# Attention products in whole float32 on halves of the array, and the first stage's normalised x one step ahead

## The chip, the cores and the metric

The kernel runs on one NeuronCore of a Trainium2 chip. The metric is device time in microseconds of one execution, as the median of several; lower is better. Engines in the rows: PE is TensorE (matmuls), PEld its weight loads, DVE is VectorE, ACT is ScalarE, POOL is GpSimd, SP is SyncE, which here only issues transfers.

## The reference

A decoder trunk of two layers over 256 tokens of width 1024, all in float32. Each layer adds half a SwiGLU feed-forward (1024 to 2816 and back), then a mixer, then another half feed-forward; every part reads an RMS-normalised x.

```python
h = h + 0.5 * swiglu(rms_norm(h, ffn1_norm[layer]), ...)
hn = rms_norm(h, mix_norm[layer])
h = h + ab_mixer(hn, ...)        # layer 0:  c_mixer(hn, ...) in layer 1
h = h + 0.5 * swiglu(rms_norm(h, ffn2_norm[layer]), ...)
...
# c_mixer: 16 heads of 64, 256 tokens are one block, so plain causal attention
q, k, v = split(x @ w_in, 3)
p = softmax(where(kpos <= qpos, q @ k.T * 64 ** -0.5, -inf))
out = (p @ v) @ w_out
```

The mixer of layer 0 has 8 heads of 64 with three dilated windows, whose outputs are combined by their softmax denominators (with 256 tokens this is one softmax with a mask that holds the logarithm of how many windows see a key), and beside them a gated branch with 128x128 position mixing; both go through one output projection.

## The kernel before, in words

The work runs on TensorE as products of float32 numbers that are cut in two: `split(hi, lo, src)` lets ScalarE round `src` to float32r (line 228, `hi`) and VectorE subtract (line 229, `lo`). A product of two cut operands is three matmuls: hi by hi, hi by lo, lo by hi (`mm3`, lines 223 to 225, and written out in `rowwise`, lines 365 to 367, `colwise`, 375 to 377, and `project`, 423 to 427). `Stream` loads every weight once from memory on SyncE's queue as a tile `raw` of 128x2048, and cuts it into `whi` (ScalarE, line 91) and `wlo` (VectorE, line 92), two pieces a tile. Three raw and four cut tiles are in flight. PSUM is eight banks of 128x512, taken by `bank()`.

The phases follow each other: feed-forward (with `begin` as the start of the first), `ab_mixer`, feed-forward, feed-forward, `c_mixer`, feed-forward. Within a phase the tile planner orders the instructions of each engine by data dependence, the program's order and its own estimates of time; `begin` alone is run under `manual_schedule`, in the order written. In a mixer the projections for q and k are computed for two heads (a pair, 128 columns) at a time; `at(slot, f, h)` puts the attention steps of head h or pair p into numbered slots between those projections, and the last slots fall into the output projection (`project`'s `after`). Layer 0 has 4 pairs, layer 1 has 8.

The steps of attention, as `make_attention` has them:
- `put_q`: for each head of the pair, q is rounded by ScalarE (line 716) into the head's own 64 rows, and VectorE's remainder (717) goes to the other 64 rows of the same tile. So q high and q low lie above each other in 128 rows.
- `put_k`: k is rounded (727) and its remainder taken (728), and GpSimd copies both to the other 64 rows (729, 730), so that kh and kl each stand twice.
- `scores`: for each head and each block of 128 queries two matmuls over 128 rows, by kh (742) and by kl (743), give (q high + q low) times k. VectorE adds the mask and takes the minimum of the negated scores (746), ScalarE takes the exponential and its sum (748), and ScalarE (755, layer 0) or GpSimd (757, layer 1) scales by the reciprocal of the sum. Only the causal part is kept: 128 keys for the first block, 256 for the second.
- `turn`: three TensorE transposes (765) put the probabilities of a head with keys in rows, and a `split` gives `pth` and `ptl`.
- `weighted`: `mm3` with v's 128 columns of the pair as the held operand and both heads' probabilities as the moving one. Each head's result is the half of the output rows that belongs to it; the other half is not used. A `split` for each head writes `mixh` and `mixl`.

V is kept as `vth` and `vtl` after a `split` of its projection.

In `begin`, the first tokens' products are made with x times gain, not yet normalised, while the norms are computed. `normed` then makes the normalised x, two slices of 128 rows at a time: VectorE multiplies (line 575), then `split` rounds on ScalarE (228) and subtracts on VectorE (229). Behind it, on the same two engines, the next weight tile is cut. Ahead of it two `colwise` products with the unnormalised `xgh`, `xgl` are ready for TensorE.

Of the kernel before, what the change touches and what calls it, by code (L numbers as in the profile page):

```python
# [140 lines left out]
def trunk(ctx: ExitStack, tc: tile.TileContext, a, out):  # L141
# [12 lines left out]
    def bank():  # L154
        return ps.tile([128, 512], F32, name="bank")
# [71 lines left out]
    def split(hi, lo, src):  # L227
        nc.scalar.activation(hi, src, AF.Copy)
        nc.vector.tensor_sub(lo, src, hi.bitcast(F32))
# [258 lines left out]
    def begin(bp, fp, pb):  # L488
# [80 lines left out]
        rs = bp.tile([128, 2, S], F32, name="rs")  # L569
        new_xT()  # L570

        def normed(k0):
            for k in range(k0, k0 + 4, 2):
                for i in range(k, k + 2):
                    nc.vector.scalar_tensor_tensor(xf[:, i, :], xf[:, i, :], gT[:, i : i + 1], rs[:, 0, :],
                                                   op0=ALU.mult, op1=ALU.mult)
                xk = xf[:, k : k + 2, :].rearrange("p k (t c) -> p k t c", t=NT)
                split(xT["h"][:, k : k + 2], xT["l"][:, k : k + 2], xk)

        pair = []  # L580
        for _ in range(2):
# [1 line left out]
            st.load_one()  # L583
        for j in range(2):
            nc.scalar.copy(rs[:, j, :], rb[:, :S])
        for m in range(2):
            normed(4 * m)
        st.split_one()
        st.load_one()
        for m in range(2):  # L590
# [111 lines left out]


    def make_attention(mp, mask_cols, nheads, v, mix, engine):
        qs, ks, probs, pts = {}, {}, {}, {}
        mask = mp.tile([128, 384], F32, name="mask")
        nc.scalar.dma_start(mask, a["consts"][:, mask_cols])

        def put_q(p, bk):

            qq = mp.tile([128, 2 * S + LINE], F32R, name="q", bufs=PAIRS)
            for j in range(2):
                q = qq[:, SHIFT + j * S : SHIFT + (j + 1) * S]
                r = slice(j * 64, j * 64 + 64)
                o = slice(64 - j * 64, 128 - j * 64)
                nc.scalar.activation(q[r, :], bk[r, :S], AF.Copy)
                nc.vector.tensor_sub(q[o, :], bk[r, :S], q[r, :].bitcast(F32))
                qs[2 * p + j] = q

        def put_k(p, bk):  # L720

            for j in range(2):
                kh = mp.tile([128, S], F32R, name=f"kh{j}", bufs=PAIRS)
                kl = mp.tile([128, S], F32R, name=f"kl{j}", bufs=PAIRS)
                r = slice(j * 64, j * 64 + 64)
                o = slice(64 - j * 64, 128 - j * 64)
                nc.scalar.activation(kh[r, :], bk[r, :S], AF.Copy)
                nc.vector.tensor_sub(kl[r, :], bk[r, :S], kh[r, :].bitcast(F32))
                nc.gpsimd.tensor_copy(kh[o, :], kh[r, :].bitcast(F32))
                nc.gpsimd.tensor_copy(kl[o, :], kl[r, :].bitcast(F32))  # L730
                ks[2 * p + j] = (kh, kl)

        def scores(h):
            q = qs.pop(h)
            kh, kl = ks.pop(h)
            sc = bank()
            pr = mp.tile([128, 384], F32, name="pr", bufs=4)
            nm = wk.tile([128, 2], F32, name="nm")
            l = wk.tile([128, 2], F32, name="l")
            for b in range(2):  # L740
                bs = slice(b * 128, b * 128 + 128)
                nc.tensor.matmul(sc[:, b * S : (b + 1) * S], q[:, bs], kh, start=True, stop=False)
                nc.tensor.matmul(sc[:, b * S : (b + 1) * S], q[:, bs], kl, start=False, stop=True)
            for b, (c0, n) in enumerate(((0, 128), (128, 256))):
                cs = slice(c0, c0 + n)
                nc.vector.tensor_tensor_reduce(pr[:, cs], sc[:, b * S : b * S + n], mask[:, cs], -SCALE, 3e38,
                                               op0=ALU.add, op1=ALU.min, accum_out=nm[:, b : b + 1])
                nc.scalar.activation(pr[:, cs], pr[:, cs], AF.Exp, bias=nm[:, b : b + 1], scale=-1.0,
                                     accum_out=l[:, b : b + 1])
            rl = wk.tile([128, 2], F32, name="rl")  # L750
            nc.vector.reciprocal(rl, l)
            for b, (c0, n) in enumerate(((0, 128), (128, 256))):
                cs = slice(c0, c0 + n)
                if engine is nc.scalar:
                    nc.scalar.activation(pr[:, cs], pr[:, cs], AF.Copy, scale=rl[:, b : b + 1])
                else:
                    engine.tensor_scalar(pr[:, cs], pr[:, cs], rl[:, b : b + 1], None, op0=ALU.mult)
            probs[h] = pr

        def turn(h):  # L760
            p, j = divmod(h, 2)
            pr = probs.pop(h)
            tp = bank()
            for i in range(3):
                nc.tensor.transpose(tp[:, i * 128 : (i + 1) * 128], pr[:, i * 128 : (i + 1) * 128], ident)
            if j == 0:
                pts[p] = [mp.tile([128, 2, 384], F32R, name=n, bufs=2) for n in ("pth", "ptl")]
            split(pts[p][0][:, j, :], pts[p][1][:, j, :], tp[:, :384])

        def weighted(p):  # L770
            o = bank().rearrange("p (j c) -> p j c", j=2)
            pth, ptl = pts.pop(p)
            vs = slice(p * 128, (p + 1) * 128)
            mm3(o, v[0][:, 0, vs], v[1][:, 0, vs], pth[:, :, :256], ptl[:, :, :256], True, False)
            mm3(o[:, :, 128:], v[0][:, 1, vs], v[1][:, 1, vs], pth[:, :, 256:], ptl[:, :, 256:], False, True)
            for j in range(2):
                r = slice(j * 64, j * 64 + 64)
                split(mix[0][r, p], mix[1][r, p], o[r, j, :].rearrange("p (t c) -> p t c", t=NT))

        return put_q, put_k, scores, turn, weighted  # L780

    def mix_tiles(mp):
        return [mp.tile([128, KD, NT, 128], F32R, name=n) for n in ("mixh", "mixl")]

    def v_tiles(mp, n):
        return [mp.tile([128, NT, n], F32R, name=m) for m in ("vth", "vtl")]

    def run_events(ev, s):
        for f in ev.pop(s, []):
# [3 lines left out]
    def ab_mixer(phase):  # L793
        with tc.tile_pool(name="mp", bufs=1) as mp:
            mix = mix_tiles(mp)
            v = v_tiles(mp, 512)
            vn = mp.tile([128, NT, 512], F32, name="vn")
            uT = mp.tile([128, 4, S], F32, name="uT")
            put_q, put_k, scores, turn, weighted = make_attention(mp, slice(0, 384), 8, v, mix, nc.scalar)
# [28 lines left out]
                        st.free()  # L828

            def keep_v(t):  # L830
                split(v[0][:, t, :], v[1][:, t, :], pb[t, 0])

            def keep_g(t):
                g = mp.tile([128, 512], F32, name="gv")
# [74 lines left out]
    def c_mixer(phase):  # L909
        with tc.tile_pool(name="mp", bufs=1) as mp:  # L910
            mix = mix_tiles(mp)
            v = v_tiles(mp, D)
            put_q, put_k, scores, turn, weighted = make_attention(mp, slice(384, 768), 16, v, mix, nc.gpsimd)
            ws, pb = {}, {}

            def block(t, m, mid=None):
                pb[t, m] = bank()
                for i in range(2):
                    if t == 0:
                        ws[m, i] = st.take()  # L920
                    rowwise(pb[t, m], t, i * 4, ws[m, i], 4)
                    if t == 1:
                        st.free()
                    if mid:
                        mid()
                cs = slice(m * 512, (m + 1) * 512)
                split(v[0][:, t, cs], v[1][:, t, cs], pb[t, m])

            ev = {}
            slot = 0  # L930

            def at(s, f, *args):
                ev.setdefault(s, []).append(lambda: f(*args))

            def step():
                nonlocal slot
                run_events(ev, slot)
                slot += 1

            for h, s in enumerate((4, 5, 6, 8, 8, 10, 11, 12, 15, 16, 17, 18, 19, 20, 20, 21)):  # L940
                at(s, scores, h)
            for h, s in enumerate((6, 7, 8, 10, 11, 12, 13, 14, 17, 18, 19, 20, 22, 22, 22, 23)):
                at(s, turn, h)
            for p, s in enumerate((9, 12, 14, 16, 20, 22, 23, 23)):
                at(s, weighted, p)

            block(0, 0)
            pend[1].turn((nc.vector, nc.scalar))
            block(1, 0)
            for c in range(4):  # L950
                if c == 2:
                    block(0, 1, step)
                    block(1, 1, step)
                for put in (put_q, put_k):
                    w = st.take()
                    for j in range(2):
                        p = bank()
                        colwise(p[:, :S], w, j)
                        put(2 * c + j, p)
                        step()  # L960
                    st.free()
            project(mix, list(range(8)), 4, 1.0, phase + 1, lambda i: step())
            assert not ev, ev.keys()
# [58 lines left out]
```

## Time and profile before

| what | value |
|---|---|
| median of 3 runs | 943.3 us (943.08 to 946.66) |
| the profiled execution, its own time | 943.16 us |
| its span, first to last instruction | 941.4 us |
| granted TensorE clock | 0.999 |
| TensorE busy | 930.4 us, 99% |
| VectorE, ScalarE, GpSimd busy | 668.3, 543.5, 176.4 us |
| memory read | 173.73 MB, 186 GB/s over the span |

A row of instructions reads: line, engine, operation, tiles written and read, shapes, count, then total busy time and the mean of one in ns, then the engine's idle time before them and what ended it. A row of waits reads: who waited, for whom, total us, times, longest. A matmul's record covers its way through the array, so records of successive matmuls overlap; the distance between starts tells how long TensorE is held. Shapes such as 128*128 are the rows and columns of the array that are used.

### The profile page before, as it was taken

The numbers are of one execution on the slowest core, as the hardware profiler recorded it, in microseconds if no ns is written. First come the engines' busy times: TensorE is split into PE (matmuls) and PEld (weight loads), VectorE is DVE, ScalarE is ACT, GpSimd is POOL, SyncE is SP. The second block draws the span as 40 slices with busy tenths as digits, with TensorE's granted clock in tenths as the row PEclk, the third lists the DMA queues.
The fourth block names the chain that finished last, engine by engine and source line by source line (L and its number), as shares of the span: only waits on it lengthen the run. The fifth ranks groups of instructions, "written<-read, shape, count | busy, mean of one in ns | idle before, by whom it ended". The sixth has DMA issues, their size and how long they took to land.

```text
span 941.4 us, 15697 instructions
## 1 busy us (share of the span) xinstructions
PE 930.4 (99%) x6320; PEld 851.3 (90%) x6320; DVE 668.3 (71%) x927; ACT 543.5 (58%) x875; POOL 176.4 (19%) x201
## 2 busy tenths in 40 slices
PE   9999999999999999999999999999999999999997
PEld 8999998889878999988889999887999889999886
DVE  6786678768766566678665667787788666567785
ACT  6664554575976445545654545457787574455451
POOL 0013312011200023121001222200446200132210
PEclk9999999999999999999999999999999999999999
DMA  9786555566434756547466654574544438664531
GB/s 329 222 281 199 180 211 180 191 206 228 134 101 155 248 180 187 175 176 262 157 207 185 207 191 156 202 241 141 196 147 135 134 122 259 197 202 144 219 135 45
DMA packets 119464, 175.78 MB, mean 187 GB/s; under 512 B 3168, under 2 KB 92384, under 8 KB 119392
## 3 DMA queue, kind: packets, MB, share of 16 engines
q1 hardware_dynamic: 117712, 172.60, 55.6%
q10 hardware_dynamic: 1680, 2.19, 0.8%
q8 instruction: 49, 0.80, 0.3%
q14 instruction: 23, 0.19, 0.1%
HBM read 173.73 MB, written 1.05 MB: 186 GB/s over the span
## 4 chain that ended last, share of the span: by engine, by line
PE 88%; ACT 5%; DVE 3%; DMA 2%; issue 1%; SPq 0%; POOL 0%; POOLq 0%; ACTq 0%; DVEq 0%
PE bank L377 16%; PE bank L376 16%; PE bank L375 16%; PE bank L427 6%; PE bank L423 6%; PE bank L424 6%; PE bank L367 4%; PE bank L365 4%; PE bank L366 4%; PE bank L223 3%; PE bank L224 3%; PE bank L225 3%; DVE wlo L92 2%; DMA raw<-in_ffn_w_up 2%; ACT whi L91 2%
## 5 line engine op out<-in xcount | busy, mean ns | idle before, releaser
L91 ACT ACTIVATE whi<-raw 128x1024 fp32r<-128x1024 f32 (+1 forms) x336 | 328.6, 1026 | 230.6 <-PE bank L376 96.3
L92 DVE TENSOR_TENSOR wlo<-raw,whi 128x1024 fp32r<-128x1024 f32 (+1 forms) x336 | 391.7, 1205 | 79.8 <-ACT whi L91 78.9
L375 PE MATMUL bank<-xTh,whi 128*128 128x256 f32 x1344 | 372.7, 277 | 0.0
L377 PE MATMUL bank<-xTh,wlo 128*128 128x256 f32 x1344 | 371.5, 276 | 0.8 <-DVE wlo L92 0.8
L376 PE MATMUL bank<-xTl,whi 128*128 128x256 f32 x1344 | 371.4, 276 | 0.0
L377 PEld LDWEIGHTS bank<-xTh,wlo 128*128 128x128 f32 x1344 | 252.3, 188 | 1.0 <-DVE wlo L92 1.0
L376 PEld LDWEIGHTS bank<-xTl,whi 128*128 128x128 f32 x1344 | 252.6, 188 | 0.1
L375 PEld LDWEIGHTS bank<-xTh,whi 128*128 128x128 f32 x1344 | 252.4, 188 | 0.2 <-ACT whi L91 0.2
L423 PE MATMUL bank<-whi,hTh 128*128 128x512 f32 x216 | 84.7, 392 | 0.0
L424 PE MATMUL bank<-wlo,hTh 128*128 128x512 f32 x216 | 84.1, 389 | 0.0
L427 PE MATMUL bank<-whi,hTl 128*128 128x512 f32 x216 | 71.1, 389 | 0.0
L365 PE MATMUL bank<-whi,xTh 128*128 128x512 f32 x160 | 63.1, 394 | 0.0
L367 PE MATMUL bank<-whi,xTl 128*128 128x512 f32 x160 | 62.5, 390 | 0.0
L366 PE MATMUL bank<-wlo,xTh 128*128 128x512 f32 x160 | 62.3, 390 | 0.0
L663 POOL TENSOR_TENSOR sil<-hm 128x128 f32<-128x128 f32 x16 | 7.4, 463 | 279.7 <-DVE hm L622 239.0
L622 DVE TENSOR_TENSOR hm<-sil,bank 128x512 f32<-128x512 f32 x35 | 24.0, 685 | 49.5 <-PE bank L377 49.5
L99 POOL TENSOR_TENSOR wx<-raw 128x512 f32<-128x512 f32 x16 | 21.9, 1371 | 172.0 <-DVE wxl L92 87.0
L235 POOL TENSOR_TENSOR rstd<-ms,half_neg 128x1 f32<-128x1 f32 x14 | 12.4, 886 | 206.9 <-DVE ms L269 202.6
L427 PEld LDWEIGHTS bank<-whi,hTl 128*128 128x128 f32 x216 | 40.5, 188 | 8.5
L424 PEld LDWEIGHTS bank<-wlo,hTh 128*128 128x128 f32 x216 | 40.6, 188 | 8.2
L423 PEld LDWEIGHTS bank<-whi,hTh 128*128 128x128 f32 x216 | 40.6, 188 | 8.2
L91 ACT ACTIVATE wxh<-wx 128x1536 fp32r<-128x1536 f32 x16 | 23.7, 1483 | 25.3 <-DVE wx L103 21.6
(172 smaller groups left out, 1282.4 us busy)
## 6 DMA issues: line engine op xcount, KB each, us to landing
raw<-in_ffn_w_down SPq DMA_DIRECT2D x44, 1024.0 KB, 5.0
raw<-in_ffn_w_gate SPq DMA_DIRECT2D x41, 1024.0 KB, 5.4
raw<-in_ffn_w_up SPq DMA_DIRECT2D x41, 1024.0 KB, 5.4
raw<-in_c_w_in SPq DMA_DIRECT2D x12, 1024.0 KB, 5.3
raw<-in_ab_w_in SPq DMA_DIRECT2D x10, 1024.0 KB, 6.3
raw<-in_ab_w_out SPq DMA_DIRECT2D x4, 1024.0 KB, 4.9
raw<-in_c_w_out SPq DMA_DIRECT2D x4, 1024.0 KB, 5.0
raw<-in_ffn_w_up SPq DMA_DIRECT2D x6, 512.0 KB, 7.0
```

Of the source, the lines that this page charges most:

```text
L91: self.nc.scalar.activation(hi, raw, AF.Copy)
L92: self.nc.vector.tensor_sub(lo, raw, hi.bitcast(F32))
L223: nc.tensor.matmul(p, sh, mh, start=start, stop=False)
L365: nc.tensor.matmul(p, xh, w[0][:, k, :], start=k0 + k == 0, stop=False)
L366: nc.tensor.matmul(p, xh, w[1][:, k, :], start=False, stop=False)
L367: nc.tensor.matmul(p, xl, w[0][:, k, :], start=False, stop=k0 + k == KD - 1)
L375: nc.tensor.matmul(p, h, xh, start=k == 0, stop=False)
L376: nc.tensor.matmul(p, h, xl, start=False, stop=False)
L377: nc.tensor.matmul(p, l, xh, start=False, stop=k == KD - 1)
L423: nc.tensor.matmul(banks[t, h], sh, w[0][:, kw, cs], start=first, stop=False)
L424: nc.tensor.matmul(banks[t, h], sh, w[1][:, kw, cs], start=False, stop=False)
L427: nc.tensor.matmul(banks[t, h], sl, w[0][:, kw, cs], start=False, stop=last)
```

## The change

Attention keeps q, k, v and the probabilities as plain float32. `put_q` is one ScalarE copy of the pair, `put_k` one VectorE copy, v one VectorE copy, and a transposed head one ScalarE copy. `scores` issues the matmuls of both heads of a pair at the even head, into two banks: for each block of queries first the head in rows 0 to 63, then the head in rows 64 to 127, with 128 keys for the first block in place of 256. `weighted` issues, for each half of the keys, one matmul for each head, whose 64 columns of v give output rows 0 to 63 or 64 to 127 of the same bank; one `split` of full height follows. The slots stay as they were.

In `begin`, `normed` runs over all eight slices, and the `split` of one pair of slices is issued after the multiplies of the next pair.

```diff
-        def normed(k0):
-            for k in range(k0, k0 + 4, 2):
-                for i in range(k, k + 2):
+        def normed():
+            for k in range(0, KD + 2, 2):
+                for i in range(k, min(k + 2, KD)):
                     nc.vector.scalar_tensor_tensor(xf[:, i, :], xf[:, i, :], gT[:, i : i + 1], rs[:, 0, :],
                                                    op0=ALU.mult, op1=ALU.mult)
-                xk = xf[:, k : k + 2, :].rearrange("p k (t c) -> p k t c", t=NT)
-                split(xT["h"][:, k : k + 2], xT["l"][:, k : k + 2], xk)
+                if k:
+                    xk = xf[:, k - 2 : k, :].rearrange("p k (t c) -> p k t c", t=NT)
+                    split(xT["h"][:, k - 2 : k], xT["l"][:, k - 2 : k], xk)
...
         def put_q(p, bk):
-            qq = mp.tile([128, 2 * S + LINE], F32R, name="q", bufs=PAIRS)
-            for j in range(2):
-                q = qq[:, SHIFT + j * S : SHIFT + (j + 1) * S]
-                r = slice(j * 64, j * 64 + 64)
-                o = slice(64 - j * 64, 128 - j * 64)
-                nc.scalar.activation(q[r, :], bk[r, :S], AF.Copy)
-                nc.vector.tensor_sub(q[o, :], bk[r, :S], q[r, :].bitcast(F32))
-                qs[2 * p + j] = q
+            qq = mp.tile([128, S + LINE], F32, name="q", bufs=PAIRS)
+            qs[p] = qq[:, SHIFT : SHIFT + S]
+            nc.scalar.copy(qs[p], bk[:, :S])
 
         def put_k(p, bk):
-            for j in range(2):
...
-                nc.scalar.activation(kh[r, :], bk[r, :S], AF.Copy)
-                nc.vector.tensor_sub(kl[r, :], bk[r, :S], kh[r, :].bitcast(F32))
-                nc.gpsimd.tensor_copy(kh[o, :], kh[r, :].bitcast(F32))
-                nc.gpsimd.tensor_copy(kl[o, :], kl[r, :].bitcast(F32))
-                ks[2 * p + j] = (kh, kl)
+            ks[p] = mp.tile([128, S], F32, name="k", bufs=PAIRS)
+            nc.vector.tensor_copy(ks[p], bk[:, :S])
 
         def scores(h):
-            q = qs.pop(h)
-            kh, kl = ks.pop(h)
-            sc = bank()
+            p, j = divmod(h, 2)
+            if j == 0:
+                q, k = qs.pop(p), ks.pop(p)
+                scs[p] = bank(), bank()
+                for b, (c0, n) in enumerate(((0, 128), (128, 256))):
+                    for i in range(2):
+                        r = slice(i * 64, i * 64 + 64)
+                        nc.tensor.matmul(scs[p][i][:, c0 : c0 + n], q[r, b * 128 : b * 128 + 128], k[r, :n],
+                                         start=True, stop=True)
+            sc = scs[p][j]
...
-            for b in range(2):
-                bs = slice(b * 128, b * 128 + 128)
-                nc.tensor.matmul(sc[:, b * S : (b + 1) * S], q[:, bs], kh, start=True, stop=False)
-                nc.tensor.matmul(sc[:, b * S : (b + 1) * S], q[:, bs], kl, start=False, stop=True)
...
-            split(pts[p][0][:, j, :], pts[p][1][:, j, :], tp[:, :384])
+            nc.scalar.copy(pts[p][:, j, :], tp[:, :384])
 
         def weighted(p):
-            o = bank().rearrange("p (j c) -> p j c", j=2)
-            pth, ptl = pts.pop(p)
-            vs = slice(p * 128, (p + 1) * 128)
-            mm3(o, v[0][:, 0, vs], v[1][:, 0, vs], pth[:, :, :256], ptl[:, :, :256], True, False)
-            mm3(o[:, :, 128:], v[0][:, 1, vs], v[1][:, 1, vs], pth[:, :, 256:], ptl[:, :, 256:], False, True)
-            for j in range(2):
-                r = slice(j * 64, j * 64 + 64)
-                split(mix[0][r, p], mix[1][r, p], o[r, j, :].rearrange("p (t c) -> p t c", t=NT))
+            o = bank()
+            pt = pts.pop(p)
+            for t, (c0, n) in enumerate(((0, 256), (256, 128))):
+                for j in range(2):
+                    r = slice(j * 64, j * 64 + 64)
+                    vs = slice(p * 128 + j * 64, p * 128 + j * 64 + 64)
+                    nc.tensor.matmul(o[r, S - n : S], v[:, t, vs], pt[:, j, c0 : c0 + n],
+                                     start=t == 0, stop=t == 1)
+            split(mix[0][:, p], mix[1][:, p], o[:, :S].rearrange("p (t c) -> p t c", t=NT))
...
-                split(v[0][:, t, :], v[1][:, t, :], pb[t, 0])
+                nc.vector.tensor_copy(v[:, t, :], pb[t, 0])
```

The same replacement of v's `split` by a copy stands in `c_mixer`.

More of the change, by code (lines that the diff above doesn't have):

```diff
@@ L585, in begin @@
             nc.scalar.copy(rs[:, j, :], rb[:, :S])
-        for m in range(2):
-            normed(4 * m)
+        normed()
         st.split_one()
@@ L704, in make_attention @@
     def make_attention(mp, mask_cols, nheads, v, mix, engine):
-        qs, ks, probs, pts = {}, {}, {}, {}
+        qs, ks, scs, probs, pts = {}, {}, {}, {}, {}
         mask = mp.tile([128, 384], F32, name="mask")
@@ L709, in put_q @@
         def put_q(p, bk):
-            qq = mp.tile([128, 2 * S + LINE], F32R, name="q", bufs=PAIRS)
-            for j in range(2):
-                q = qq[:, SHIFT + j * S : SHIFT + (j + 1) * S]
-                r = slice(j * 64, j * 64 + 64)
-                o = slice(64 - j * 64, 128 - j * 64)
-                nc.scalar.activation(q[r, :], bk[r, :S], AF.Copy)
-                nc.vector.tensor_sub(q[o, :], bk[r, :S], q[r, :].bitcast(F32))
-                qs[2 * p + j] = q
-        def put_k(p, bk):
-            for j in range(2):
-                kh = mp.tile([128, S], F32R, name=f"kh{j}", bufs=PAIRS)
-                kl = mp.tile([128, S], F32R, name=f"kl{j}", bufs=PAIRS)
-                r = slice(j * 64, j * 64 + 64)
[L726 to L730, printed above, removed]
-                ks[2 * p + j] = (kh, kl)
-        def scores(h):
-            q = qs.pop(h)
-            kh, kl = ks.pop(h)
-            sc = bank()
+            qq = mp.tile([128, S + LINE], F32, name="q", bufs=PAIRS)
+            qs[p] = qq[:, SHIFT : SHIFT + S]
+            nc.scalar.copy(qs[p], bk[:, :S])
+        def put_k(p, bk):
+            ks[p] = mp.tile([128, S], F32, name="k", bufs=PAIRS)
+            nc.vector.tensor_copy(ks[p], bk[:, :S])
+        def scores(h):
+            p, j = divmod(h, 2)
[8 more added lines that the diff above has]
+            sc = scs[p][j]
             pr = mp.tile([128, 384], F32, name="pr", bufs=4)
@@ L739, in scores @@
             l = wk.tile([128, 2], F32, name="l")
-            for b in range(2):
-                bs = slice(b * 128, b * 128 + 128)
-                nc.tensor.matmul(sc[:, b * S : (b + 1) * S], q[:, bs], kh, start=True, stop=False)
-                nc.tensor.matmul(sc[:, b * S : (b + 1) * S], q[:, bs], kl, start=False, stop=True)
             for b, (c0, n) in enumerate(((0, 128), (128, 256))):
                 cs = slice(c0, c0 + n)
-                nc.vector.tensor_tensor_reduce(pr[:, cs], sc[:, b * S : b * S + n], mask[:, cs], -SCALE, 3e38,
+                nc.vector.tensor_tensor_reduce(pr[:, cs], sc[:, cs], mask[:, cs], -SCALE, 3e38,
                                                op0=ALU.add, op1=ALU.min, accum_out=nm[:, b : b + 1])
@@ L766, in turn @@
             if j == 0:
-                pts[p] = [mp.tile([128, 2, 384], F32R, name=n, bufs=2) for n in ("pth", "ptl")]
-            split(pts[p][0][:, j, :], pts[p][1][:, j, :], tp[:, :384])
+                pts[p] = mp.tile([128, 2, 384], F32, name="pt", bufs=2)
+            nc.scalar.copy(pts[p][:, j, :], tp[:, :384])
         def weighted(p):
-            o = bank().rearrange("p (j c) -> p j c", j=2)
-            pth, ptl = pts.pop(p)
-            vs = slice(p * 128, (p + 1) * 128)
-            mm3(o, v[0][:, 0, vs], v[1][:, 0, vs], pth[:, :, :256], ptl[:, :, :256], True, False)
-            mm3(o[:, :, 128:], v[0][:, 1, vs], v[1][:, 1, vs], pth[:, :, 256:], ptl[:, :, 256:], False, True)
-            for j in range(2):
-                r = slice(j * 64, j * 64 + 64)
-                split(mix[0][r, p], mix[1][r, p], o[r, j, :].rearrange("p (t c) -> p t c", t=NT))
+            o = bank()
[7 more added lines that the diff above has]
+            split(mix[0][:, p], mix[1][:, p], o[:, :S].rearrange("p (t c) -> p t c", t=NT))
         return put_q, put_k, scores, turn, weighted
@@ L783, in mix_tiles, with v_tile @@
         return [mp.tile([128, KD, NT, 128], F32R, name=n) for n in ("mixh", "mixl")]
-    def v_tiles(mp, n):
-        return [mp.tile([128, NT, n], F32R, name=m) for m in ("vth", "vtl")]
+    def v_tile(mp, n):
+        return mp.tile([128, NT, n], F32, name="vt")
     def run_events(ev, s):
@@ L795, in ab_mixer @@
             mix = mix_tiles(mp)
-            v = v_tiles(mp, 512)
+            v = v_tile(mp, 512)
             vn = mp.tile([128, NT, 512], F32, name="vn")
@@ L911, in c_mixer @@
             mix = mix_tiles(mp)
-            v = v_tiles(mp, D)
+            v = v_tile(mp, D)
             put_q, put_k, scores, turn, weighted = make_attention(mp, slice(384, 768), 16, v, mix, nc.gpsimd)
@@ L926, in block @@
                 cs = slice(m * 512, (m + 1) * 512)
-                split(v[0][:, t, cs], v[1][:, t, cs], pb[t, m])
+                nc.vector.tensor_copy(v[:, t, cs], pb[t, m])
             ev = {}
```

## The prediction

> **What bounds the kernel now.** I read the page first: engine totals, then the chain that ended last.
>
> ```profile
> PE 930.4 (99%) x6320; PEld 851.3 (90%) x6320; DVE 668.3 (71%) x927; ACT 543.5 (58%) x875; POOL 176.4 (19%) x201
> ...
> PE 88%; ACT 5%; DVE 3%; DMA 2%; issue 1%; SPq 0%; POOL 0%; POOLq 0%; ACTq 0%; DVEq 0%
> ```
>
> TensorE is busy 930.4 of 941.4 us and carries 88% of the chain. So two things can move the end: the time that TensorE's own matmuls take, and the few places where it waits. Work taken from ScalarE, VectorE or GpSimd counts only at those places. The next view is the busy time by stretches of 10 us, where I looked for stretches with PE below 10.00 in the two attentions (the first at 233 to 275 us, the second at 665 to 748 us).
>
> ```profile
> 240.00:250.00 10.00, 9.93 (x75) 8.96 (x74) 8.11 (x21) 9.80 (x28) 1.30 (x4) 1.00 0.41 121
> 250.00:260.00 10.00, 9.53 (x54) 8.13 (x54) 7.02 (x23) 8.57 (x23) 1.95 (x5) 1.00 0.55 197
> 260.00:270.00 10.00, 9.05 (x44) 6.72 (x43) 7.94 (x18) 9.21 (x23) 0.00 (x0) 1.00 0.32 105
> ...
> 720.00:730.00 10.00, 9.77 (x66) 8.44 (x66) 9.00 (x24) 7.54 (x19) 9.22 (x12) 1.00 0.33 107
> ...
> 740.00:750.00 10.00, 9.91 (x47) 7.66 (x46) 5.78 (x10) 4.38 (x9) 0.00 (x0) 1.00 0.47 154
> ```
>
> The columns are PE, PEld, DVE, ACT, POOL, then the granted clock (1.00) and the DMA. PE is idle 0.07 + 0.47 + 0.95 = 1.49 us in the first attention, with ScalarE at 9.80, 8.57 and 9.21 of 10, and 0.23 + 0.09 = 0.32 us in the second, with VectorE at 9.00 and GpSimd at 9.22 beside the larger part. All else there is TensorE at work. What ended its waits, from the waits of 225 to 270 us (first five rows) and of 690 to 750 us (the rest):
>
> ```profile
> PEld bank L765 <- ACT pr L755: 1.4, 3, 0.9
> PE bank L765 <- ACT pr L755: 0.6, 1, 0.6
> PE bank L742 <- DVE ptl L229: 0.5, 1, 0.5
> PEld bank L224 <- DVE ptl L229: 0.4, 1, 0.4
> PEld bank L423 <- DVE ptl L229: 0.4, 1, 0.4
> ...
> PEld bank L223 <- DVE kl L728: 0.5, 1, 0.5
> ...
> PEld bank L742 <- POOL kh L729: 0.3, 1, 0.3
> ```
>
> Transposes wait for the normalised probabilities from ScalarE; matmuls wait for the low halves of the probabilities and of k from VectorE and GpSimd, directly or because VectorE still holds a bank.
>
> **The change, part by part.**
>
> *1. What a float32 matmul costs.* The old kernel has one whole-float32 product of two data tiles, the spatial mixing at L861. The timeline shows two of its calls between ordinary matmuls.
>
> ```profile
> 217.55 0.28 PE L377 MATMUL bank<-xTh,wlo 128*128 128x256 f32 x1
> ...
> 217.89 0.28 PE L377 MATMUL bank<-xTh,wlo 128*128 128x256 f32 x1
> 218.01 0.60 PE L861 MATMUL bank<-wsT,vn 128*128 128x128 f32 x4
> 218.37 0.37 PE L375 MATMUL bank<-xTh,whi 128*128 128x256 f32 x1
> 218.57 0.28 PE L376 MATMUL bank<-xTl,whi 128*128 128x256 f32 x1
> ```
>
> Two calls leave four records: each call runs as two passes. A record (0.28) is longer than the distance between starts, because matmuls overlap in the pipeline; starts are what counts. L377 comes round every three matmuls, 217.55 and 217.89: 0.113 us for each. From L377 at 217.89 to L376 at 218.57 is 0.68; less two ordinary steps that is 0.454 for four passes, 0.1135 per pass of 128 columns. A float32r matmul needs the same for 256 columns. So a float32 pass costs twice as much per column, and a call is two passes: 128 columns 0.227 us, 256 columns 0.454.
>
> *2. Scores.* Before, a head takes four float32r matmuls; after, a pair takes four float32 calls, (128 + 256 columns) for each row half. Before, from the timeline:
>
> ```profile
> 239.79 0.28 PE L742 MATMUL bank<-kh,q 128*128 128x256 f32 x1
> ...
> 240.24 0.28 PE L375 MATMUL bank<-xTh,whi 128*128 128x256 f32 x1
> ```
>
> 0.45 per head, 0.90 per pair. After, if the two halves run one behind the other: 2 x (0.227 + 0.454) = 1.36 per pair. If they run fully side by side: 0.68. No record here uses a part of the array, so these are the bounds: -0.22 to +0.46 per pair. What I take lies between. TensorE starts its matmuls in the order of the program (every timeline above). A call's second pass has to wait for its first, on the same half; so it can run beside the first pass of the next call, on the other half, and the overlap goes no further. In order that gives 0.113 + 0.113 + 0.227 + 0.227 + 0.227 = 0.907: no gain, no loss. Each pass also has its own weight load of 128 columns; were those loads (one per 0.113 us step above) to hold the other half back, it would be up to 1.11.
>
> *3. Weighted sums.* Before, one pair from the timeline:
>
> ```profile
> 257.31 0.39 PE L223 MATMUL bank<-pth,vth 128*128 128x512 f32 x1
> ...
> 258.36 0.40 PE L423 MATMUL bank<-whi,mixh 128*128 128x512 f32 x1
> ```
>
> 1.05 us for six matmuls, half of whose products are thrown away. After, four float32 calls (two of 256, two of 128 columns, alternating column halves): 1.36 one behind the other, 0.68 side by side, and by the one-ahead order 3 x 0.227 + 2 x 0.113 = 0.908. So -0.37 to +0.31 per pair; I take -0.14. There are 12 pairs (4 + 8): scores 0, weighted -1.7 us. The bounds over both: 12 x (-0.59) = -7.1 and 12 x (+0.77) = +9.2 us.
>
> The Trainium skill, "TensorE: Matmul & The Clock Gate", Part 3, says that matmuls on different parts of the array run concurrently and start and end in program order, and measured 3.07x for four row tiles and 2.38x for three column tiles. As an estimate from that page, two halves at about 1.55x would make a group 1.36 / 1.55 = 0.88 and the sum 12 x (-0.02 - 0.17) = -2.3 us; no run here shows it yet.
>
> *4. Work off the other engines.* Rows by shape, removed first, then the nearest rows for what is added:
>
> ```profile
> L716 ACT ACTIVATE q<-bank 64x256 fp32r<-64x256 f32 x24 | 9.1, 379 | 6.3 <-DVE q L717 5.4 <-PE bank L377 0.6
> L727 ACT ACTIVATE kh<-bank 64x256 fp32r<-64x256 f32 x24 | 9.1, 380 | 6.8 <-DVE kl L728 6.4
> L228 ACT ACTIVATE mixh<-bank 64x256 fp32r<-64x256 f32 x24 | 9.0, 376 | 9.9 <-DVE mixl L229 7.7 <-PE bank L225 2.1
> L717 DVE TENSOR_TENSOR q<-bank,q 64x256 fp32r<-64x256 f32 x24 | 10.1, 422 | 1.8 <-ACT q L716 1.2
> L728 DVE TENSOR_TENSOR kl<-bank,kh 64x256 fp32r<-64x256 f32 x24 | 10.1, 421 | 1.9 <-ACT kh L727 1.3
> L229 DVE TENSOR_TENSOR ptl<-bank,pth 128x384 fp32r<-128x384 f32 x24 | 13.0, 552 | 2.3 <-ACT pth L228 1.9
> L229 DVE TENSOR_TENSOR mixl<-bank,mixh 64x256 fp32r<-64x256 f32 x24 | 10.1, 420 | 7.1 <-ACT mixh L228 7.0
> L729 POOL CAST kh<-kh 64x256 fp32r<-64x256 f32 x24 | 12.5, 522 | 51.4 <-ACT kh L727 50.7
> L730 POOL CAST kl<-kl 64x256 fp32r<-64x256 f32 x24 | 12.2, 508 | 5.7 <-DVE kl L728 4.9
> ...
> L585 ACT COPY rs<-bank 128x256 f32<-128x256 f32 x2 | 0.6, 366 | 0.0
> L228 ACT ACTIVATE mixh<-tmp 128x256 fp32r<-128x256 f32 x4 | 1.7, 418 | 3.9 <-DVE tmp L867 3.8
> L229 DVE TENSOR_TENSOR mixl<-tmp,mixh 128x256 fp32r<-128x256 f32 x4 | 1.7, 426 | 1.5 <-ACT mixh L228 1.4
> ```
>
> Per pair ScalarE loses 2 x (379 + 380 + 376) and gains a copy (366) and a split of full height (418): -1.49 us. VectorE loses 2 x (422 + 421 + 552 + 420) and gains two of 426: -2.78. GpSimd loses 2 x (522 + 508) = -2.06. Over 12 pairs: ScalarE -18, VectorE -33, GpSimd -25 us. V is copied once by VectorE; its ScalarE half goes. Nearly all of this lies beside matmuls and is worth nothing there. It is worth something at the waits of 1.49 + 0.32 = 1.8 us. A record outlasts its step by 0.28 - 0.113 = 0.16, so each wait costs that more than the idle time shows; the nine waits in the rows above make 1.8 + 9 x 0.16 = 3.2 us. The rows behind `ptl`, `kl` and `kh` lose their cause, since a transposed head is now one ScalarE copy and k one VectorE copy; the transposes behind L755 stay on ScalarE's chain, which gets shorter by about 3 of its 27.6 us in 240 to 270. I take three quarters: -2.4 us, between 0 and -3.2. Late next is L755 itself, exp and scaling of the last heads.
>
> What it costs elsewhere: the even head now takes two score banks at once, and the odd head's stays held until its own slot. While the output projection holds four of eight banks, two for scores, one for a transpose and one for a weighted sum make eight, so the next request waits for a softmax. The row L742 <- `ptl` (0.5 us) is that kind of wait; a bank is now returned 0.55 us sooner (no `ptl`), which covers it. Softmax of an even head starts after both heads' matmuls, about 0.45 us later, and the odd head's needs no matmul any more. The tile planner orders by its own estimates and may order other work differently; I put that at nothing, with 1 us either way.
>
> *5. Normalised x a step ahead.* DVE and PE at the end of the first stage:
>
> ```profile
> 36.75 0.87 DVE L575 SCALAR_TENSOR_TENSOR xf<-xf,gT,rs 128x256 f32<-128x256 f32 x2
> 38.32 0.69 DVE L229 TENSOR_TENSOR xTl<-xf,xTh 128x512 fp32r<-128x512 f32 x1 [0.70 <-ACT xTh L228]
> 39.27 2.36 DVE L92 TENSOR_TENSOR wlo<-raw,whi 128x1024 fp32r<-128x1024 f32 x2 [0.26 <-ACT whi L91]
> ...
> 39.52 0.28 PE L376 MATMUL bank<-xTl,whi 128*128 128x256 f32 x1
> ...
> 40.55 0.38 PE L377 MATMUL bank<-xTh,wlo 128*128 128x256 f32 x1 [0.76 <-DVE wlo L92]
> ```
>
> In each of four rounds VectorE multiplies two slices, idles 0.70 while ScalarE rounds them, then subtracts. With the next multiply put in that gap, about 3 x 0.70 = 2.1 us go, and the weights' low half (39.27) starts near 37.2 instead and ends near 38.4, before TensorE wants it at 39.63. ScalarE's part follows the same multiplies and comes as much earlier. The step from 39.52 to 40.55 shrinks from 1.03 to 0.11: -0.9, and the record of 40.55 is 0.10 longer than the usual 0.28, which goes too: -1.0 us. No DMA is moved; the weights' next load is issued after the same split, earlier.
>
> *Sum.* Scores 0, weighted -1.7, waits -2.4, first stage -1.0: -5.1 us. The profiled execution took 943.16 us (span 941.4), and the median of the runs is 943.3, so the two are one: 943.2 - 5.1 = **938.1 us**. Its own range: weight loads binding in the scores (+2.4) and half the relief (+1.2) above, the full relief (-0.8) and the planner (-1) below: 936 to 942.
>
> **The rivals.**
>
> *Full overlap of the halves.* Both groups at 0.68: 12 x (-0.59) = -7.1, waits and first stage as above -3.4: 932.7 us. For it: half the array is idle in either half's pass. Against it: in-order starts, and a second pass that must follow the first on its half.
>
> *No overlap (the change doesn't do what it says; slower).* Both groups at 1.36: +9.2 - 3.4 = +5.8, 949.0 us. For it: no record here shows matmuls on two parts of the array at once. Against it: nothing in the trace either, so it keeps a full share. It decides from the point where a pair's scores and weighted sum together take over 0.28 us more than now (12 x 0.28 = 3.4, what the other terms give).
>
> *Emptying the pipeline at each change between whole and half array.* A matmul's record outlasts its step by 0.16 us. If the array must run empty before its division changes, that is lost twice for each group: 12 pairs x 2 groups x 2 x 0.163 = 7.8 us, so 938.1 + 7.8 = 945.9 us. For it: half and whole arrays alternate 24 times here. Against: the change from float32r to float32 at 217.89 is within the 0.1135 per pass, with no such loss. The Trainium skill, "TensorEngine Tiling (Array Packing)", Key Properties, states that changing the tiling mode drains TensorE; no record of this trace can show it.
>
> **How the numbers follow.** The forecast gets 0.42, full overlap 0.18, no overlap 0.20, emptying 0.20. A measurement of this kernel can tell about 0.5%, 4.7 us, from no change, so faster is below 938.5 and slower above 948.0. The forecast lies on that edge: 0.26 of its 0.42 faster, 0.16 the same; full overlap is faster; emptying is the same for most of it (0.12), a tenth split at both sides (0.03 faster, 0.05 slower); no overlap 0.06 the same and 0.14 slower. Sum: faster 0.47, same 0.34, slower 0.19. The range, 931 to 949, reaches to full overlap below and no overlap above; outside it are no overlap with emptying, and more relief than the waits show.
>
> **What would show it.** Two records for each float32 call at 64 rows or 64 columns; starts on the two halves at the same time, or 0.113 and 0.227 apart. A pair's scores near 0.9 and its weighted sum near 0.9 us by starts; 1.36 means no overlap, about 0.33 more at each group emptying. PE nearer 10.00 in 240 to 270 and 720 to 750. No `wlo` wait before L377 at 40 us. I am wrong if the groups exceed 1.1 us, or if PE's idle time in the attentions grows because two score banks are wanted at once.

## The result, and the profile after

The changed kernel takes 938.33 us (median; 938.19 to 938.55) against 943.27 before: ratio 0.9945, interval 0.9927 to 0.9964. The forecast was 938.1. Its profiled execution has a span of 936.5 us against 941.4. The time fell as forecast, but two terms of the sum did not come out as forecast, and it is luck that they offset each other. Each can be read in the profile.

The first part of the page, and its chain that ended last:

```profile
PE 927.4 (99%) x6344; PEld 842.1 (90%) x6344; DVE 634.9 (68%) x855; ACT 521.1 (56%) x821; POOL 150.3 (16%) x153
...
PE 97%; DVE 1%; issue 1%; ACT 1%; POOL 0%; POOLq 0%; DVEq 0%; ACTq 0%
```

TensorE's share of the chain went from 88% to 97%. VectorE, ScalarE and GpSimd lost 33, 22 and 26 us, as the rows promised (V's rounding on ScalarE included). The stretches in which TensorE had been idle:

```profile
240.00:250.00 10.00, 10.00 (x79) 9.03 (x77) 6.81 (x16) 8.53 (x21) 0.00 (x0) 1.00 0.47 156
250.00:260.00 10.00, 10.00 (x64) 7.18 (x63) 6.14 (x24) 7.88 (x25) 0.00 (x0) 1.00 0.40 114
260.00:270.00 10.00, 10.00 (x56) 7.54 (x55) 3.97 (x6) 6.42 (x16) 0.00 (x0) 1.00 0.53 172
720.00:730.00 10.00, 10.00 (x59) 7.36 (x60) 6.02 (x24) 7.40 (x22) 5.81 (x8) 1.00 0.44 150
740.00:750.00 10.00, 10.00 (x49) 7.99 (x48) 3.62 (x9) 4.51 (x13) 0.57 (x1) 1.00 0.33 107
```

TensorE is busy 10.00 of 10 in all five; since a matmul's record (0.28 us) outlasts its step (0.113), a full 10.00 does not say that every step is an ordinary one. Where the time went is told best by stages. The first transpose L327 of each new norm is a landmark that both kernels have, so each trace is cut at its starts in the timeline:

| stage | before, us | after, us | difference |
|---|---|---|---|
| start to the turn into the first mixer | 183.49 | 182.83 | -0.66 |
| first mixer, to the turn behind it | 95.16 | 91.38 | -3.78 |
| two feed-forwards | 359.53 | 359.51 | 0.0 |
| turn of the second mixer's x (token half 0 to half 1) | 9.83 | 10.42 | +0.59 |
| second mixer | 105.07 | 103.99 | -1.08 |
| rest | 188.33 | 188.34 | 0.0 |

Now the two groups of matmuls themselves, from the timeline of the changed kernel, a group of scores and then a weighted sum:

```profile
232.65 0.28 PE L377 MATMUL bank<-xTh,wlo 128*128 128x256 f32 x1
232.85 0.93 PE L728 MATMUL bank<-k,q 64*128 64x128 f32 x8
233.71 0.39 PE L375 MATMUL bank<-xTh,whi 128*128 128x256 f32 x1
233.93 0.28 PE L376 MATMUL bank<-xTl,whi 128*128 128x256 f32 x1
...
265.48 0.39 PE L427 MATMUL bank<-whi,mixl 128*128 128x512 f32 x1
265.79 0.87 PE L767 MATMUL bank<-pt,vt 128*64 128x256 f32 x8
266.59 0.50 PE L423 MATMUL bank<-whi,mixh 128*128 128x512 f32 x1
266.93 0.40 PE L424 MATMUL bank<-wlo,mixh 128*128 128x512 f32 x1
```

As in the prediction: from the start of the last whole-array matmul to the start of the second one behind the group, less two ordinary steps. Scores: 1.28 - 2 x 0.113 = 1.05 us, where the old pair took 0.90. Weighted sum: 1.45 - 2 x 0.227 = 1.00, where the old one took 1.05. Within a group the starts repeat in the other groups of this trace to about 0.01 us. So TensorE's attention work did not shrink by 1.7 us; it grew by 12 x (0.15 - 0.05) = 1.2 us. The two mixers got shorter by 4.86 all the same, so, as the difference, 6.1 us of waits went.

### The profile page after: what moved, and what is told of

Read it like the earlier page. It is cut to its first block, busy times and chain, and to the rows that moved or that the text cites. A ratio compares the mean times of both kernels' runs of the same rounds, so it can differ in the third digit from the quotient of the medians.

```text
span 936.5 us, 15524 instructions
## 1 busy us (share of the span) xinstructions
PE 927.4 (99%) x6344; PEld 842.1 (90%) x6344; DVE 634.9 (68%) x855; ACT 521.1 (56%) x821; POOL 150.3 (16%) x153
## 3 DMA queue, kind: packets, MB, share of 16 engines
HBM read 173.73 MB, written 1.05 MB: 187 GB/s over the span
## 4 chain that ended last, share of the span: by engine, by line
PE 97%; DVE 1%; issue 1%; ACT 1%; POOL 0%; POOLq 0%; DVEq 0%; ACTq 0%
PE bank L375 17%; PE bank L376 17%; PE bank L377 17%; PE bank L423 7%; PE bank L427 7%; PE bank L424 7%; PE bank L365 4%; PE bank L367 4%; PE bank L366 4%; PE bank L223 3%; PE bank L224 3%; PE bank L225 3%; PE bank L728 1%; PE bank L767 1%; PE bank L755 1%; PE bank L327 1%
## 5 line engine op out<-in xcount | busy, mean ns | idle before, releaser
L377 PE MATMUL bank<-xTh,wlo 128*128 128x256 f32 x1344 | 371.4, 276 | 0.0
L376 PE MATMUL bank<-xTl,whi 128*128 128x256 f32 x1344 | 371.3, 276 | 0.0
L376 PEld LDWEIGHTS bank<-xTl,whi 128*128 128x128 f32 x1344 | 252.6, 188 | 0.1
L377 PEld LDWEIGHTS bank<-xTh,wlo 128*128 128x128 f32 x1344 | 252.3, 188 | 0.0
```

What stands on the lines that cost most here:

```text
L376: nc.tensor.matmul(p, h, xl, start=False, stop=False)
L377: nc.tensor.matmul(p, l, xh, start=False, stop=k == KD - 1)
```

## Experiments

*Is it the halves, and in what order?* The matmuls of a group in another order: both calls of one half, then both of the other.

```diff
-                for b, (c0, n) in enumerate(((0, 128), (128, 256))):
-                    for i in range(2):
+                for i in range(2):
+                    for b, (c0, n) in enumerate(((0, 128), (128, 256))):
...
-            for t, (c0, n) in enumerate(((0, 256), (256, 128))):
-                for j in range(2):
+            for j in range(2):
+                for t, (c0, n) in enumerate(((0, 256), (256, 128))):
```

> The changed kernel with the matmuls of a group in another order: both calls of the first half of the array, then both of the second; same calls, same results. Theory A (neighbouring calls on different halves run fully side by side, 0.68 us for a group of 1.36 us of passes): 24 groups lose 0.68 us each where no neighbours differ, at most 938.3 + 16.3 = 954.6 us; one overlap at the seam may give back 0.1 to 0.2 us a group. Theory B (the forecast: only a second pass runs beside the next first pass): one overlap in place of three, about 0.3 us a group, 945 us. Theory C (each half works off its own queue, whatever the order): 938.3 us.

It took 938.89 us (937.9 to 939.21): the order does not matter, theory C. The tile planner did not simply put the old order back: in this trace the second half's first pass starts 0.013 us behind the first half's, in nearly every group, and in the changed kernel 0.007. In its trace, the records of L728 in the stretch from 233.2 to 233.5 us, the first 0.24 us of a group, and in the stretch that ends 0.2 us later:

```profile
L728 PE MATMUL bank<-k,q x4: 272/322/373, 233.3 to 233.5; 64*128 64x128 f32 x4
...
L728 PE MATMUL bank<-k,q x6: 272/373/378, 233.3 to 233.6; 64*128 64x128 f32 x4, 64*128 64x256 f32 x2
```

By 233.5 all four passes of 128 columns have started and none of 256, though the program issues the first half's 256-column call ahead of the second half's 128-column call. So each half of the array works off its own calls, and a later call overtakes an earlier one of the other half. The Trainium skill, "TensorE: Matmul & The Clock Gate", Part 3, says that matmuls start and end strictly in program order; these records do not agree, and the measurement decides. By the one-ahead order of the forecast this kernel would have been about 7 us slower.

*What is paid for the division?* Each group twice in a row, the same values:

```diff
-                for b, (c0, n) in enumerate(((0, 128), (128, 256))):
+                for b, (c0, n) in 2 * [(0, (0, 128)), (1, (128, 256))]:
...
-            for t, (c0, n) in enumerate(((0, 256), (256, 128))):
+            for t, (c0, n) in 2 * [(0, (0, 256)), (1, (256, 128))]:
```

> The changed kernel with every group of scores and of weighted sums issued twice in a row into the same banks (the same values twice). Theory A (0.68 us for the passes, and the rest of the 1.06 and 1.01 us per group is paid once for entering and leaving the divided array): + 24 x 0.68 = 16.3 us, 954.6 us, and the second round starts without a gap. Theory B (the forecast: a group's passes themselves take 0.91 us or more, nothing is paid for the division): + 24 x 0.91 to 1.03 = 22 to 25 us, 960 to 963 us.

It took 953.88 us: 15.5 us more than the changed kernel for 24 more rounds, 0.65 a round. The timeline of one group of scores:

```profile
232.42 0.28 PE L377 MATMUL bank<-xTh,wlo 128*128 128x256 f32 x1
232.63 1.58 PE L728 MATMUL bank<-k,q 64*128 64x128 f32 x16
234.14 0.39 PE L375 MATMUL bank<-xTh,whi 128*128 128x256 f32 x1
234.36 0.28 PE L376 MATMUL bank<-xTl,whi 128*128 128x256 f32 x1
```

1.94 from L377 to L376 against 1.28 above: the second round costs 0.66. That is the 0.68 of full overlap. The rest of a group, 1.05 - 0.66 = 0.39 for scores and 1.00 - 0.65 = 0.35 for a weighted sum, is paid once for going in and coming out, about 0.18 for each change. The waits of the weight loads in the changed kernel name the place:

```profile
PEld bank L755 <- issue: 2.0, 6, 0.3
...
PEld bank L375 <- issue: 1.8, 7, 0.3
PEld bank L767 <- issue: 1.7, 8, 0.4
PEld bank L728 <- issue: 1.4, 4, 0.4
PEld bank L423 <- issue: 1.4, 7, 0.4
```

"issue" is idle time that nothing in the profile ended. 8.3 us of it stand before the first weight load behind a change; the old kernel has no such rows. In an ordinary stream the next weights load while a matmul runs: the load for the L377 at 232.65 starts at 232.54. Behind a change they do not: the group's first load starts at 232.85, with its matmul. The Trainium skill, "TensorEngine Tiling (Array Packing)", Key Properties, says that changing the tiling mode drains TensorE, and that different tiles can load weights and multiply in parallel: both agree with these runs, with about 0.18 us a change and 0.65 of 1.36 us a group.

*One half of attention at a time.* Only q, k and scores as in the changed kernel (the rest of attention as before), and only transposed probabilities, v and weighted sums; both with the new first stage. The code of each side is that of the diff above.

> The kernel before with the first stage a step ahead and only q, k and the scores in whole float32 on row halves; transposed probabilities, v and weighted sums as before. Theory A (scores cost TensorE 12 x 0.15 = 1.8 us more; the 6 us of waits come about half from each side): 943.3 - 1.2 + 1.8 - 3 = 940.9 us. Theory D (the waits hang on the low halves of the probabilities alone): no relief here, 943.9 us.

> The changed kernel with q, k and the scores as before; transposed probabilities, v and weighted sums in whole float32 on column halves. Theory A (weighted sums cost TensorE 12 x 0.04 = 0.5 us less; half of the 6 us of waits go): 943.3 - 1.2 - 0.5 - 3 = 938.6 us. Theory D (all the relief is on this side): 935.6 us, below the changed kernel.

939.32 us (ratio to before 0.9959, 0.9947 to 0.9972) and 939.22 us (0.9959, same interval). By stages the first mixer takes 92.70 and 92.66 us (95.16 before, 91.38 with both), the second 104.41 and 103.79 (105.07, 103.99). The scores alone end below both of their expected figures, the weighted sums alone above both of theirs: the waits do not divide into two halves. Either side alone brings 2.5 of the first mixer's 3.8 us, so the two share waits that either of them removes. Theory D, that all hangs on the low halves of the probabilities, falls. In the second mixer the weighted side alone is even 0.2 us shorter than both: there the scores on halves cost TensorE 8 x 0.15 = 1.2 us, slightly more than what they bring.

*Load, or the length of the chain?* Idle work of the old size put back on ScalarE, VectorE and GpSimd, first beside the chain (results that nobody reads), then in it (operands rewritten in place with their own values, and the transposed bank held by VectorE):

```diff
+            d = mp.tile([128, 384], F32R, name="dt", bufs=2)              # beside
+            nc.vector.tensor_sub(d, pts[p][:, j, :], mask)
...
+            nc.vector.tensor_sub(pts[p][:, j, :], tp[:, :384], zero)      # in the chain
```

and in the same manner for q, k and the weighted sum.

> The changed kernel with idle work put on ScalarE (1.5 us a pair), VectorE (2.8) and GpSimd (2.1) at the places where the old splits and copies stood, written to tiles that nobody reads: the engines carry the old load, the steps of attention do not wait for it except in their queues. Theory A (the gain is the engines' load, through the in-order queues): 3 to 6 us come back, 941 to 944 us, with TensorE waiting again for probabilities and transposes. Rival (the gain is the shorter chain itself: no remainder to wait for, banks freed sooner): under 1.5 us, below 939.8 us.

> The changed kernel with the old amount of work on ScalarE, VectorE and GpSimd put back in the steps themselves: q, k and the transposed probabilities are rewritten in place with their own values before they are used, the transposed bank is held by a VectorE instruction as before, and a weighted sum is split by halves. Theory E (in the first mixer the gain is the shorter chain from bank to operand, which work beside the chain did not bring back): 943 to 944.5 us, the first mixer 3 to 4 us longer than in the changed kernel. Rival (the same load is what counts, in the chain or beside it): 941.9 us, as with the work beside it.

Beside the chain: 941.88 us, 3.5 us of the 5 come back. The stages tell them apart: first mixer 92.47 (+1.1), second 106.41 (+2.4, more than it had gained). In the second it is GpSimd's queue in this run; the weight loads' waits from 650 to 752 us of that kernel:

```profile
PEld bank L772 <- POOL pr L764: 3.1, 4, 1.0
```

The transposes (there L772) wait for GpSimd's scaling (L764), which stands behind the idle copies. So load beside the chain is enough to make TensorE wait in the second mixer. It is not shown that GpSimd made the old waits. All three engines got their load back at once. GpSimd got more than it had: from 648 to 750 us it is busy 54.3 us, against 44.8 in the kernel before and 26.4 in the changed one. And the old waits there were shorter and for other tiles (the rows from 690 to 750 us in the prediction name `kl` and `kh`, at most 0.5 us each). In the chain: 946.23 us, the first mixer 95.72 (+4.3) and the second 107.91 (+3.9). That is over both expectations. Its waits from 225 to 275 us show why:

```profile
PE bank L748 <- POOL k L738: 1.9, 1, 1.9
...
PE bank L775 <- ACT pr L765: 0.3, 1, 0.3
```

Rewriting k on three engines one after the other makes a longer chain to the scores than the old kernel had. So this run shows that the first mixer answers to the chain's length (1.1 us for load beside it, 4.3 with it inside); it does not show the size of the old chain's part.

*The first stage alone, and attention alone.* Each is one side of the diff on the kernel before.

> The kernel before with only the first stage's normalised x made a step ahead; attention as before. Theory A (the one wait near 40 us goes and nothing takes its place): the wait of 0.9 us before L377 and its refilling vanish, 943.3 - 1.2 = 942.1 us. Rival (the stall moves to the next weight tile or its load): 943.3 us, with a new wait of about 1 us between 40 and 60 us.

> The changed kernel with the first stage as before; attention in whole float32. Theory A (TensorE's attention work grew by about 1.3 us, and about 6 us of waits went): 938.3 + 1.2 = 939.5 us. Rival (the two edits help each other): clearly more or less than 1 us from 938.3.

The first stage alone: 942.41 us, ratio 0.9976 (0.9963 to 0.9988), 0.7 us faster than the 943.14 beside it; expected -1.2. The kernel before and the changed kernel where TensorE turns to the normalised x:

```profile
39.05 0.28 PE L377 MATMUL bank<-xgh,wlo 128*128 128x256 f32 x1
39.29 0.38 PE L375 MATMUL bank<-xTh,whi 128*128 128x256 f32 x1
...
40.77 0.28 PE L375 MATMUL bank<-xTh,whi 128*128 128x256 f32 x1
...
39.70 0.28 PE L377 MATMUL bank<-xgh,wlo 128*128 128x256 f32 x1
39.81 0.28 PE L375 MATMUL bank<-xTh,whi 128*128 128x256 f32 x1
...
40.15 0.28 PE L375 MATMUL bank<-xTh,whi 128*128 128x256 f32 x1
```

Before, the four steps from 39.05 to 40.77 take 1.72 us, 1.27 more than four ordinary ones; in the changed kernel (39.70 to 40.15) nothing is left of that. But that kernel's profile gained only 0.66 to the first mark. Its opening matmuls, run to raise the clock, took longer than before:

```profile
L486 PE MATMUL bank<-warm 128*128 128x128 f32 x28 | 5.7, 397 | 1.1 <-DVE warm L214 1.1
```

(4.8 us and 347 ns before.) In the traces the full clock is granted from 4.03 us on before, and from 6.05 us on in the changed kernel. So the first matmul behind them starts at 6.60 us in place of 5.63. In the fourteen profiles of these runs that start lies between 5.63 and 6.96 us, whatever the kernel; it hides part of the gain. The old wait also differs between executions: three profiles with the old first stage and the new attention (below) lose 0.55, 0.89 and 0.70 us in the same four steps. So 1.27 is this one profile's, and 0.7 is what the medians of the runs show.

Attention alone: 941.84 us, ratio 0.9969 (0.9953 to 0.9985), with runs from 938.52 to 943.68. Expected was 939.5; by the median this is the rival's outcome, since the two parts alone bring 0.7 and 1.3 us and both together 4.9. The profiled execution was the shortest, 938.52. A second and a third run were to catch a long execution in a profile:

> The kernel with only attention changed, once more, for a profile of one of its longer executions (its runs spread from 938.5 to 943.7 us, those of kernels with the new first stage by under 2 us). Theory F (the first stage's late low half sometimes makes TensorE wait more than the 0.5 us of the profile at hand, and what follows is late too): 941 us or more, with the excess before 60 us. Rival (the spread is in the attention): the excess lies after 183 us.

> The kernel with only attention changed, a third time, to catch a longer execution in a profile. Theory F (the first stage's late low half): 941 us or more, with the excess over the earlier profile before 60 us. Rival (the spread is in the attention): the excess lies after 183 us. At 938 to 939 us it tells nothing.

They gave 938.94 and 939.52 us (the latter 0.9928 of the kernel before, 0.9899 to 0.9957, with all three of its runs beside it near 946): no long one was caught. The kernel before has runs near 946 as well as near 943, a spread of 4.6 us; no kernel with the new first stage spreads by more than 2.4 us. That points at the late first stage, which would make the two parts help each other, but what happens in the long executions stays open.

*The wait that grew.* The second mixer's turn, VectorE in the kernel before (first two rows), then VectorE and TensorE in the changed kernel:

```profile
646.27 1.28 DVE L92 TENSOR_TENSOR wlo<-raw,whi 128x512 fp32r<-128x512 f32 x2
647.47 0.48 DVE L307 TENSOR_SCALAR xn<-x,rstd 128x512 f32<-128x512 f32 x1
...
641.81 1.28 DVE L92 TENSOR_TENSOR wlo<-raw,whi 128x512 fp32r<-128x512 f32 x2
643.01 0.68 DVE L918 COPY vt<-bank 128x512 f32<-128x512 f32 x1
643.61 0.47 DVE L307 TENSOR_SCALAR xn<-x,rstd 128x512 f32<-128x512 f32 x1
...
644.14 1.09 PE L327 MATMUL bank<-ident,xn 128*128 128x128 f32 x8 [1.69 <-DVE xn L307]
```

V's copy has no ScalarE step to wait for any more, so it stands ahead of the scaling that TensorE waits for.

```diff
-                nc.vector.tensor_copy(v[:, t, cs], pb[t, m])
+                nc.scalar.copy(v[:, t, cs], pb[t, m])
```

> The changed kernel with v's copy in the second mixer on ScalarE in place of VectorE. Theory A (the wait of TensorE for the normalised half row at the start of the second mixer, which grew from 1.48 to 2.08 us between starts, grew because the copy stands ahead of that scaling in VectorE's queue): about 0.6 us less, 937.7 us, and the step back at 1.5 us or under. Rival (the scaling waits for GpSimd's root, not for the copy): 938.3 us, step unchanged.

937.78 us, ratio 0.9944 (0.9931 to 0.9958), with the turn back at 9.82 us from 10.42:

```profile
642.88 1.09 PE L327 MATMUL bank<-ident,xn 128*128 128x128 f32 x8 [1.11 <-DVE xn L307]
```

*Fewer changes of the array.* On top of that, the scores of two neighbouring pairs as one group: all four couples of the second mixer, the first couple of the first.

```diff
-            if j == 0:
-                q, k = qs.pop(p), ks.pop(p)
-                scs[p] = bank(), bank()
+            if p not in scs:
+                both = range(p, p + (2 if nheads == 16 or p == 0 else 1))
+                for g in both:
+                    scs[g] = bank(), bank()
+                for g in both:
+                    q, k = qs.pop(g), ks.pop(g)
...
```

> The changed kernel with v's copy on ScalarE in the second mixer, and the scores of two neighbouring pairs issued as one group into four banks (all four such couples of the second mixer, the first of the first mixer). Theory A (entering and leaving the divided array costs 0.38 us a group of scores, whatever is in it): five groups fewer, 937.8 - 5 x 0.38 = 935.9 us. Rival (four score banks of eight held until four softmaxes have read them make TensorE wait for a bank): 937.8 us or more, with waits of TensorE on the mask's reading of the scores.

936.25 us, ratio 0.9926 (0.9914 to 0.9938), the best kernel here. The second mixer went from 104.04 to 102.65 us, 0.35 for each of four groups, near the 0.38 expected; the first from 91.41 to 91.29, less than expected for its one group. No wait for a bank is among TensorE's.

## Why the prediction was right

The total was within 0.3 us, by terms that were not: attention on TensorE came out 2.9 us worse than forecast and the waits 3.7 us better. That they cancel is luck. For the two profiled executions:

| term | forecast, us | measured, us | from |
|---|---|---|---|
| scores on TensorE | 0 | +1.8 | 12 x (1.05 - 0.90) |
| weighted sums on TensorE | -1.7 | -0.6 | 12 x (1.00 - 1.05) |
| waits in the mixers | -2.4 | -6.1 | stages -4.86, less the two above |
| first stage | -1.0 | -1.3 | four steps at 39 to 41 us; 0.7 by the medians |
| opening matmuls and the steps just behind them | 0 | +0.6 | first mark -0.66, less the row above |
| turn of the second mixer | 0 | +0.6 | stage 9.83 to 10.42 |
| sum | -5.1 | -5.0 | span -4.9 |

- *A float32 pass costs twice per column*: right. Two rounds in a row run at 0.65 a round, the 0.68 of the side-by-side bound.
- *The halves overlap one pass ahead*: wrong. The step that failed is "TensorE starts its matmuls in the order of the program": true of whole-array rows, the only ones there were, not of parts: the second half's first pass starts 0.007 us behind the first half's, before the first call's second pass. Full overlap was the rival with 0.18.
- *No price for the division*: wrong; that rival had 0.163 us for each change, and 0.18 was measured. Full overlap and emptying are both true. Together they give 0.68 + 0.37 = 1.05, which lies only 0.14 above the forecast's 0.91 by chance. They should not have been counted as alternatives.
- *The waits*: the mechanism was right, load off ScalarE, VectorE and GpSimd counts only where TensorE waits. The term was mis-sized, at 2.4 for 6.1 us, and its upper bound of 3.2 us was too small as well. That bound took the waits that the rows name, with 0.16 us more for each (one of them stands there twice: the matmul's 0.6 us before L765 and its weight load's 0.9). What those rows don't name was left out; the 6.1 us is a difference of stages, and it is not shown wait by wait.
- *The two score banks*: right, no bank wait came.
- *The first stage*: right in kind and near in size. The wait went, nothing took its place; that the opening matmuls differ between executions was not in the sum.
- *Late next is L755*: not so; in the profile after, no wait of TensorE's matmuls in the first attention is left. What came late was V's copy ahead of the scaling in the second mixer, "VectorE loses work" read without asking what moves up in its queue.

## What to carry to other kernels

On a TensorE-bound kernel, sum the steps between starts of matmuls, not the idle time of their records: the difference to the ordinary step is the whole of what the waits cost, and here it was about twice what the idle time and the named waits showed. Parts of the array do run fully side by side, but each change between whole and divided costs a visible part of a short group, so gather the divided matmuls into few, long groups. And an operation that no longer waits for another engine can move ahead in its own engine's queue, as V's copy did: look at what it pushes back.

## What was not expected of the hardware

Calls on different halves of the array overtake each other: with one half's two calls issued first, the other half still started 0.013 us behind it, and the kernel took 938.89 us in place of 938.33. A change between the whole and the divided array costs about 0.18 us, and the first weights behind it are not loaded ahead. The time at which the opening matmuls, run to raise the clock, are done differs from run to run: 5.63 to 6.96 us in fourteen profiles.
